# Conditioning vector spread by full-row products, first chunk's rows unsplit, output stores on other queues

## The chip, the cores and the metric

The kernel runs on one core of a Trainium2 chip. A core has a matrix engine (TensorE, PE in the profile; its weight loads are listed apart as PEld), a vector engine (VectorE, DVE), a scalar engine (ScalarE, ACT), a general engine (GpSimd, POOL) and a queueing engine (SyncE, SP). Transfers are issued on the queues of SP and ACT and carried by 16 DMA engines. The metric is the device time of one execution in microseconds (us), taken as the median of several runs.

## The reference

A decoder trunk of two layers over 256 tokens of width 1024, in float32. Each layer runs a half-step SwiGLU feed-forward block (FFN), a token mixer (attention in layer 0, a gated linear recurrence in layer 1) and a second FFN. Each of these sub-layers normalises its input and modulates it by a conditioning vector `c`:

```python
c_act = silu(c)
mod = (c_act @ mod_w[layer] + mod_b[layer]).reshape(B, 3, 3, D)
shift, scale, gate = mod[:, j, 0], mod[:, j, 1], mod[:, j, 2]
h = rmsnorm(x, g) * (1 + scale) + shift
x = x + w * (1 + gate) * sublayer(h)
```

Nothing of the first FFN can start before `silu(c)`, the first rows of `mod_w`, the row sums of squares of `x` and the first weights are there.

## The kernel before

**Layout.** `x` is kept transposed: eight chunks of 128 features by 256 tokens. Weights arrive in float32, and ACT and DVE split each piece into a high part `wh` (ACT copy, line 586) and a low part `wl` (DVE subtraction, line 589); PE then makes three products for each 128x128 block, high times high, high times low, low times high (line 616). Only the first chunk of the first FFN (k = 0) is multiplied unsplit, by float32 products (line 945).

**The order of the work.** Every operation is first recorded with a cost, its reads and its writes; `schedule` then makes one order for each engine from these costs and due times, and the program is issued in that order. Each engine executes its list in order, so an operation that waits holds all behind it on its engine. Loads go out on SP's queue in a written order (`first_order`): the two halves of `x`, then for each chunk k of the first FFN the rows of `mod_w` for scale (`m1`) and shift (`m0`) and the FFN's weights (`gu`). `m1`, `m0` and `gu` of a chunk are 512 KB, 512 KB and 1 MB.

**The head.** The first 13 us run as follows. PE fills the time with products of zeros (`warm`, line 1464: six at first, one in the middle, nine late). The conditioning vector comes by ACT's queue into `rawm`, as 8 rows of 128 numbers (`CR = 8`). PE spreads it over all 128 partitions: eight float32 products, each of one column of an identity matrix (`unit`, held at 8 rows) with the 8 rows (line 1481), four into each of two PSUM banks; ACT takes silu of each bank into one half of `cact` (512 columns). ACT and DVE square and add `x`; PE sums over the partitions with a matrix of ones (line 714); ACT makes `rms` by a logarithm and `rst` by an exponential.

Each row block of `mod_w` is multiplied by `cact` and summed along its row by one DVE instruction (line 650, 1024 columns, followed by a read of the accumulator). For k = 0 this is done in halves (`first_row`, line 916): two DVE instructions of 512 columns for `m1` and two for `m0`; ACT joins each pair (one instruction turns the first half's sum and the bias into `parts`, one adds the second half's sum). The result is the scale `mf` of chunk 0 and its shift.

Then DVE makes `hpre`, which is `x` times scale times `rst` (line 739), and a second tensor with the shift added (line 744, for the unsplit products: the two scalars are `parts` and the second half's raw sum). PE starts line 945, 16 logical products that the profile shows as 32 matmuls. ACT and DVE meanwhile make the split chunk 0 (`hx`) and all further chunks (lines 954, 967 and 969), for the products of k = 1 to 7 at line 616.

**The end.** After the last sub-layer PE sums the squares (line 1417) and ACT and DVE normalise the two halves of 128 tokens; DVE writes six pieces (lines 1434 and 1440), and each piece is stored when it is ready, by SP's queue (line 1445) or by ACT's (line 554), as the table `PUTS` says (half, first chunk, chunks, queue).

Of the kernel before, what the change touches and what calls it, by code (L numbers as in the profile page):

```python
# [39 lines left out]
EARLY, MID, LATE = 6, 1, 9  # L40
AHEAD = {(1, 0): 3}
KICK0, COPIED, PLAIN = (1, 4), (7,), 2
HXPAD, HKPAD, ARPAD = 112, 16, 88
SKIP = 1
PUTS = ((0, 0, 2, "SP"), (0, 2, 3, "SP"), (0, 5, 3, "SP"), (1, 0, 3, "ACT"), (1, 3, 3, "SP"), (1, 6, 2, "ACT"))
CR = 8
SCORES = 1450.0
VALUES = 1400.0

# [333 lines left out]
def first_order():  # L383

    yield "x", 0, 0, 4 * T
    yield "x", 4, 0, 4 * T + NP0
    for k in range(KD):
        for w in ("m1", "m0"):
            for a in range(0, D, D // 2 if k == 0 else D):
                yield w, k, a, D // 2 if k == 0 else D  # L390
        for a, n in zip(starts(k), pieces(k)):
            yield "gu", k, a, n

# [18 lines left out]
def trunk(ctx, tc, first_in, cb, par, modw, gu, wdn, qk, wv, wo, win, wri, wout, out):  # L412
# [88 lines left out]
    def fixed(name, cols, dt=F32):  # L501
        return const.tile([P, cols], dt, tag=name, name=name)
# [2 lines left out]
    x = [Buf(ap=xall[:, d * T : (d + 1) * T]) for d in range(KD)]  # L505
    cact = Buf(ap=fixed("cact", D))
    pars = Buf(ap=xall[:, KD * T :])
    zero = fixed("zero", 2 * P, BF16)
    pool.memset(zero, 0.0)
    eps_t = fixed("eps", 1)  # L510
# [10 lines left out]
    ident = fixed("ident", P, BF16)  # L521
    mask = fixed("mask", P)
    pool.affine_select(at[1][:, :P], ones, [[1, P]], ALU.is_equal, 0.0, base=0, channel_multiplier=-1)
    unit = at[1]
    dve.tensor_copy(ident, at[1][:, :P])
    pool.memset(mask, -NEG)
    pool.affine_select(mask, mask, [[1, P]], ALU.is_gt, NEG, base=0, channel_multiplier=-1)
# [8 lines left out]
    def col(off, n=1):  # L536
        return pars()[:, off : off + n]
# [4 lines left out]
                mraw[l, q, w] = Buf(ap=fixed(f"mr{l}{q}{w}", KD))  # L542
                mfin[l, q, w] = Buf(ap=fixed(f"mf{l}{q}{w}", KD))
    gbias = Buf(ap=fixed("gbias", KD))
    parts0 = [Buf(ap=fixed(f"parts{w}", 2)) for w in range(2)]
    shr = {(l, q): Buf(ap=fixed(f"sh{l}{q}", 2 * KD, F32R)) for l in range(2) for q in range(3) if l or q}
    fixed("pad1", ARPAD)

# [4 lines left out]
    def act_dma(dst, src, r, w, lat=2600.0):  # L553
        return pr.op("ACT", 60.0, lambda: act.dma_start(dst(), src() if callable(src) else src), r, w, lat=lat)
# [6 lines left out]
    def V(fn, n, r, w, cost=None, ptr=0, after=()):  # L561
        return pr.op("DVE", cost or c_dve(n) + 62.0 * ptr, fn, r, w, after)
# [171 lines left out]
    def norm_chunk(gen, d, q, whole=False):  # L734
        gs, sh = mfin[gen + (1,)], mfin[gen + (0,)]
        hp, hi, lo = Buf(hpr), Buf(hxr), Buf(hxr)
        hcur.setdefault(gen, []).append((hi, lo))
        c = slice(d, d + 1)
        V(lambda: dve.scalar_tensor_tensor(hp(), x[d](), gs()[:, c], q(), ALU.mult, ALU.mult), T,  # L739
          [x[d], (gs, d), q], [hp], ptr=1)  # L740
        h = None
        if whole:
            h, p, m = Buf(hpr), parts0[0], mraw[gen + (0,)]
            V(lambda: dve.tensor_scalar(h(), hp(), p()[:, 1:2], m()[:, c], ALU.add, ALU.add), T, [hp, (p, 1), (m, d)], [h], ptr=1)
        A(lambda: hi()[:, :T], hp, AF.Identity, T, [hp, (sh, d)], [hi], ptr=1, bias=lambda: sh()[:, c])
        V(lambda: dve.scalar_tensor_tensor(lo()[:, :T], hp(), sh()[:, c], f32(hi()[:, :T]), ALU.add, ALU.subtract), T,
          [hp, (sh, d), hi], [lo], ptr=1)
        lows[gen] = pr.ops[-1]
        return h
# [139 lines left out]
    def ffn(l, s, nxt, hook):  # L889
# [12 lines left out]
        if j == 0:  # L902
# [4 lines left out]

            gb, goff, boff = gbias, OFF_NG, OFF_MB

            def first_row(w):  # L910

                raw, m, f, p = Buf(rows, 8), mraw[0, 0, w], mfin[0, 0, w], parts0[w]
                for h in range(2):
                    cs, o = slice(h * D // 2, (h + 1) * D // 2), p if h == 0 else m
                    chained(lambda cs=cs: raw()[:, cs], at_[f"m{w}", 0, h * D // 2], D // 2, [(raw, h)], RATE0)
                    V(lambda cs=cs, o=o: dve.scalar_tensor_tensor(raw()[:, cs], raw()[:, cs], 1.0, cact()[:, cs], ALU.mult, ALU.mult,
                                                                  accum_out=o()[:, :1]),
                      D // 2, [(raw, h), (cact, h)] + [gbias] * (w == 1), [(raw, h), (o, 0)])
                    g = w == 1
                    first = lambda: gbias()[:, :1] if g else col(boff)  # L920
                    A(lambda h=h: f()[:, :1] if h else p()[:, 1:2], lambda o=o: o()[:, :1], AF.Identity, 1,
                      [(o, 0), (pars, 0), gbias] + [(p, 1)] * h, [(f, 0) if h else (p, 1)], ptr=1 + g,
                      scale=(lambda: col(goff)) if g else 1.0, bias=(lambda: p()[:, 1:2]) if h else first)

            def early(k, w):

                if k == KD:
                    return
                if k == 0:
                    first_row(w)  # L930
                    return
                last[:] = [mod_tile(0, 0, w, k, last, LAT0 if k < 3 + w else LAT1, RATE0, Buf(rows, 8))]
                m, f = mraw[0, 0, w], mfin[0, 0, w]
                mk, fk = (lambda: m()[:, k : k + 1]), (lambda: f()[:, k : k + 1])
                if w == 1:
                    A(fk, mk, AF.Identity, 1, [(m, k), (pars, 0), gb], [(f, k)], ptr=2, scale=lambda: col(goff + k),
                      bias=lambda: gb()[:, k : k + 1])
                else:
                    A(fk, mk, AF.Identity, 1, [(m, k), (pars, 0)], [(f, k)], ptr=1, bias=lambda: col(boff + k))
# [515 lines left out]
    def chained(dst, src, n, w, rate=RATE, lat=LAT0):  # L1455
        last[:] = [dma(dst, src, n, w, last, lat, rate)]
# [9 lines left out]

    def first_loads(F):
        c, b = Buf(modr), [Buf(banks), Buf(banks)]
        act_dma(lambda: c()[:CR, : D // CR], cb.rearrange("o (r n) -> (o r) n", r=CR), [], [c], 300.0)

        def cond(h, after=()):
            cs = slice(h * 512, (h + 1) * 512)
            A(lambda: cact()[:, cs], b[h], AF.Silu, 512, [b[h]], [(cact, h)], table="silu", psum=True, after=after)

        warm(EARLY)
        cw = D // CR
        for h in range(2):
            def fn(h=h):
                for r in range(h * CR // 2, (h + 1) * CR // 2):
                    o = r * cw - h * 512  # L1480
                    pe.matmul(b[h]()[:, o : o + cw], unit[:CR, r : r + 1].to_broadcast([CR, P]), c()[:CR, :cw], start=o == 0,  # L1481
                              stop=True, skip_group_check=True)
            pr.op("PE", 1870.0, fn, [c], [b[h]])
        warm(MID, [pr.last_pe])

        sq = [Buf(F, 8), Buf(F, 8)]
        extra = (0, NP0)
        tiles = {}
        for h in range(2):
            d, a0, n = 4 * h, 4 * h * T, 4 * T + extra[h]  # L1490
            chained(lambda a0=a0, n=n: xall[:, a0 : a0 + n], at_["x", d, 0], n, x[d : d + 4] + [(pars, 0)] * h, RATE0)

        def on_act(h, i):
            q, d = sq[h], 4 * h + i
            tiles[d] = (q, slice(i * T, (i + 1) * T), i)
            return A(lambda: q()[:, i * T : (i + 1) * T], x[d], AF.Square, T, [x[d]], [(q, i)])

        def on_dve(h, i):
            q, d = sq[h], 4 * h + i
            for e in range(2):  # L1500
                tiles[d + e] = (q, slice((i + e) * T, (i + e + 1) * T), "V")
            V(lambda: dve.tensor_tensor(q()[:, i * T : (i + 2) * T], xall[:, d * T : (d + 2) * T], xall[:, d * T : (d + 2) * T],
                                        ALU.mult), 2 * T, x[d : d + 2], [(q, "V")])

        on_dve(0, 2)
        on_act(0, 0)
        cond(0, [on_act(0, 1)])
        p, one = Buf(F, 4), Buf(F, 2)
        V(lambda: dve.tensor_tensor(p(), sq[0]()[:, : 2 * T], sq[0]()[:, 2 * T :], ALU.add), 2 * T,
          [(sq[0], "V"), (sq[0], 0), (sq[0], 1)], [p])  # L1510
        fold = V(lambda: dve.tensor_tensor(one(), p()[:, :T], p()[:, T:], ALU.add), T, [p], [one])
        on_dve(1, 0)
        on_act(1, 2)
        cond(1, [on_act(1, 3)])
        two = Buf(F, 2)
        V(lambda: dve.tensor_tensor(two(), sq[1]()[:, :T], sq[1]()[:, T : 2 * T], ALU.add), T, [(sq[1], "V")], [two])
        pairs = [tiles[6], (one, slice(0, T), None), tiles[7], (two, slice(0, T), None)]
        ssq[0, 0] = tuple(pairs)
        pr.op("DVE", 80.0, lambda: dve.scalar_tensor_tensor(gbias(), col(OFF_MB + KD, KD), 1.0, col(OFF_NG, KD), ALU.add,
                                                            ALU.mult), [(pars, 0)], [gbias], [fold])  # L1520
# [98 lines left out]
```

## Time and profile before

| what | value |
|---|---|
| median of 3 runs | 947.25 us (946.97 to 947.35) |
| the profiled execution, its own time | 946.62 us |
| its span, first to last instruction | 944.9 us |
| PE busy | 936.1 us, 99% of the span |
| DVE busy | 780.2 us, 83% |
| ACT busy | 559.9 us, 59% |
| first product of the first FFN (line 945) | starts at 12.61 us |
| last product | starts at 937.75 us |

A row of the profile names line, engine, operation and tiles (`out<-in`), then the count, the busy time and the mean duration. Matmuls overlap, so the duration of one is longer than the distance to the next. In the view that lists instructions in order of time a row begins with start and duration in us, and runs of the same instruction are merged (`x16`). The view of stretches gives for each engine the busy time and, in brackets, the number of instructions, then the clock granted to PE (1.00 or 0.50), the busy share of the DMA engines and their rate. That clock column holds recorded changes only; before the first of them it prints 1.00.

### The profile page before, as it was taken

Reading aid. Unit: us, or ns where it says so; the run is one execution under the profiler, and the core shown is the slowest. Engines: PE = TensorE matmul, PEld = TensorE weight load, DVE = VectorE, ACT = ScalarE, POOL = GpSimd, SP = SyncE. Lnnn points to the kernel's source line nnn. Section 1 sums busy time; section 2 is a strip of 40 time slices with the busy share of each in tenths; the row PEclk is TensorE's granted clock in tenths of the full one; section 3 lists DMA queues with packets and bytes.
Section 4 is the critical chain, followed back from the end, with each engine's and each line's share of the span. In section 5 each row is a group of like instructions: output and inputs, shape, how many; then the busy total and the mean of one; then the engine's idle time right before and its main releaser. Section 6 shows DMA issues by size and latency. Waiting matters only on the chain.

```text
span 944.9 us, 19631 instructions
## 1 busy us (share of the span) xinstructions
PE 936.1 (99%) x8092; PEld 926.9 (98%) x8092; DVE 780.2 (83%) x1250; ACT 559.9 (59%) x923; POOL 2.1 (0%) x14
## 2 busy tenths in 40 slices
PE   9999999999999999999999999999999999999997
PEld 7999999999999999999999999999999999999996
DVE  7999988799978998888899998866999997555444
ACT  6785453488776754554376544535789685544343
POOL 0000000000000000000000000000000000000000
PEclk9999999999999999999999999999999999999998
DMA  9989899947852888889967988886333656555531
GB/s 361 404 328 358 320 359 356 364 181 297 288 201 93 302 337 320 314 322 354 361 264 278 359 332 331 325 334 222 137 128 142 223 183 245 197 184 204 169 114 45
DMA packets 48777, 251.24 MB, mean 266 GB/s; under 512 B 5416, under 2 KB 6320, under 8 KB 28976
## 3 DMA queue, kind: packets, MB, share of 16 engines
q1 hardware_dynamic: 48384, 249.66, 71.0%
q8 instruction: 63, 1.03, 0.4%
q10 hardware_dynamic: 304, 0.33, 0.1%
q14 instruction: 26, 0.21, 0.1%
HBM read 248.92 MB, written 1.05 MB: 265 GB/s over the span
## 4 chain that ended last, share of the span: by engine, by line
PE 99%; DVE 0%; ACT 0%; issue 0%; POOL 0%; DVEq 0%; ACTq 0%; POOLq 0%
PE bank L616 92%; PE bank L1070 2%; PE bank L1303 1%; PE bank L945 1%; PE bank L1136 1%; PE bank L1197 1%; PE bank L1173 1%; PE bank L1481 0%; PE bank L714 0%; DVE raw L1434 0%; PE bank L1176 0%; PE bank L1464 0%; PE bank L1417 0%; PE bank L706 0%; ACT rms L558 0%
## 5 line engine op out<-in xcount | busy, mean ns | idle before, releaser
L616 PE MATMUL bank<-hx,wh 128*128 128x256 f32 (+1 forms) x3264 | 559.5, 277 | 0.0
L586 ACT ACTIVATE wh<-raw 128x1024 fp32r<-128x1024 f32 (+1 forms) x330 | 337.1, 1039 | 287.5 <-PE bank L616 213.8
L616 PEld LDWEIGHTS bank<-hx,wh 128*128 128x128 f32 x3264 | 493.0, 188 | 0.0
L589 DVE TENSOR_TENSOR wl<-raw,wh 128x1024 fp32r<-128x1024 f32 (+1 forms) x330 | 388.3, 1197 | 125.1 <-ACT wh L586 120.7
L616 PE MATMUL bank<-hx,wl 128*128 128x256 f32 (+1 forms) x1640 | 452.4, 277 | 0.0
L616 PEld LDWEIGHTS bank<-hx,wl 128*128 128x128 f32 x1640 | 308.1, 188 | 0.0
L616 PE MATMUL bank<-arenar,wh 128*128 128x256 f32 x1696 | 289.4, 276 | 0.0
L616 PEld LDWEIGHTS bank<-arenar,wh 128*128 128x128 f32 x1696 | 255.2, 188 | 0.3 <-issue 0.3
L616 PE MATMUL bank<-arenar,wl 128*128 128x256 f32 x848 | 234.2, 276 | 0.0
L616 PEld LDWEIGHTS bank<-arenar,wl 128*128 128x128 f32 x848 | 159.2, 188 | 0.1
L650 DVE SCALAR_TENSOR_TENSOR rawm<-rawm,cact 128x1024 f32<-128x1024 f32 x128 | 154.5, 1219 | 3.9 <-DMA rawm<-in_modw 3.8
L558 ACT ACTIVATE arenar<-a 128x256 fp32r<-128x256 f32 x88 | 35.3, 405 | 7.7 <-DVE a L882 7.6
L887 DVE TENSOR_TENSOR arenar<-a,arenar 128x256 fp32r<-128x256 f32 x88 | 36.4, 419 | 0.5 <-ACT arenar L558 0.5
L882 DVE TENSOR_TENSOR a<-bank,sg 128x256 f32<-128x256 f32 x82 | 34.1, 418 | 1.6 <-ACT sg L558 1.3
L558 ACT ACTIVATE sg<-bank 128x256 f32<-128x256 f32 x82 | 30.0, 369 | 7.2 <-PE bank L616 7.1
L558 ACT ACTIVATE arenaf<-bank 128x256 f32<-128x256 f32 (+1 forms) x53 | 22.9, 487 | 12.2 <-DVE bank L1146 4.5
L794 DVE SCALAR_TENSOR_TENSOR x<-bank,mf,x 128x256 f32<-128x256 f32 (+1 forms) x49 | 21.8, 473 | 9.1 <-PE bank L616 9.1
L558 ACT ACTIVATE hx<-x,mf 128x256 fp32r<-128x256 f32 x40 | 19.2, 502 | 15.6 <-DVE x L794 15.6
L558 ACT ACTIVATE hx<-hpre,mf 128x256 fp32r<-128x256 f32 x41 | 20.0, 503 | 8.4 <-DVE hpre L739 8.2
L1070 PE MATMUL bank<-wh,hx 128*128 128x256 f32 x128 | 23.5, 281 | 0.0
L1559 ACT ACT_TABLE_LOAD x15 | 19.2, 1283 | 1.6 <-PEq L1607 1.4
L1070 PEld LDWEIGHTS bank<-wh,hx 128*128 128x128 f32 x128 | 20.1, 189 | 0.1
(131 smaller groups left out, 510.6 us busy)
## 6 DMA issues: line engine op xcount, KB each, us to landing
raw<-in_gu SPq DMA_DIRECT2D x79, 1024.0 KB, 4.8
rawm<-in_modw SPq DMA_DIRECT2D x128, 512.0 KB, 6.5
raw<-in_wdn SPq DMA_DIRECT2D x44, 1024.0 KB, 5.1
raw<-in_win SPq DMA_DIRECT2D x10, 1024.0 KB, 4.8
raw<-in_qk SPq DMA_DIRECT2D x8, 1024.0 KB, 4.9
arenar<-in_first_in SPq DMA_DIRECT2D x14, 512.0 KB, 8.4
raw<-in_wout SPq DMA_DIRECT2D x5, 1024.0 KB, 4.9
raw<-in_first_in SPq DMA_DIRECT2D x8, 512.0 KB, 8.9
```

What stands on the lines that cost most here:

```text
L558: act.activation(o(), i(), f, **{k: (v() if callable(v) else v) for k, v in kw.items()})
L586: act.activation(h()[:, :m], raw()[:, a : a + m], AF.Copy)
L589: dve.tensor_tensor(lo()[:, :m], raw()[:, a : a + m], f32(h()[:, :m]), ALU.subtract)
L616: pe.matmul(o(b())[:, c], wc(u()), xc(v())[:, c], start=start and n == 0, stop=stop and n == len(passes) - 1, skip_group_check=True)
L650: dve.scalar_tensor_tensor(raw(), raw(), 1.0, cact(), ALU.mult, ALU.mult, accum_out=m()[:, t : t + 1])
L794: dve.scalar_tensor_tensor(x[d]()[:, w], acc.b()[:, j * T + w.start : j * T + w.stop], gate()[:, d : d + 1], x[d]()[:, w], ALU.mult, ALU.add)
L882: V(lambda: dve.tensor_tensor(a(), b()[:, T:], sg(), ALU.mult), T, [(b, (1, 0)), sg], [a])
L887: V(lambda: dve.tensor_tensor(y[1](), a(), f32(y[0]()), ALU.subtract), n, [a, y[0]], [y[1]])
L945: pr.op("PE", c_mm(T, 4), lambda: pe.matmul(b()[:, g * T : (g + 1) * T], raw()[:, c0 : c0 + P], h0(), start=start, stop=False, skip_group_ ...
L1070: pe.matmul(o, u()[:, tb * P : (tb + 1) * P], v()[:, c0 : c0 + 256], start=start and n == 0, stop=k == KD - 1 and n == 2, skip_group_check ...
L1136: pe.matmul(zb[e][i]()[:, j * m : (j + 1) * m], y()[rows, kc], y()[rows, qc], start=j == 0, stop=j == 1, skip_group_check=True)
L1559: act.preload_act_table_set(TABLES[t])
```

## The change

Five edits.

- The conditioning vector is loaded as one row of 1024 numbers into the last partition of its tile. DVE sets the other 127 partitions of that tile to zero ahead of everything else on its list. PE spreads the vector with two float32 products of the full 128-row matrix of ones, 512 columns each, in place of eight products of 8 rows and 128 columns.
- For k = 0, `m1` and `m0` are loaded whole (one transfer of 512 KB each in place of two of 256 KB) and reduced by one DVE instruction of 1024 columns each, with one ACT instruction behind each, like the other chunks. `first_row` and its `parts` tiles go.
- Line 744 keeps its shape, but adds the raw sum of `m0` and the bias column as its two scalars.
- A padding tile grows by 16 columns where the `parts` tiles went.
- The stores of four of the six output pieces change queues. The order by piece was SP, SP, SP, ACT, SP, ACT and becomes SP, SP, ACT, SP, ACT, SP.

```diff
-HXPAD, HKPAD, ARPAD = 112, 16, 88
+HXPAD, HKPAD, ARPAD = 112, 16, 104
-PUTS = ((0, 0, 2, "SP"), (0, 2, 3, "SP"), (0, 5, 3, "SP"), (1, 0, 3, "ACT"), (1, 3, 3, "SP"), (1, 6, 2, "ACT"))
-CR = 8
+PUTS = ((0, 0, 2, "SP"), (0, 2, 3, "SP"), (0, 5, 3, "ACT"), (1, 0, 3, "SP"), (1, 3, 3, "ACT"), (1, 6, 2, "SP"))
...
-        for w in ("m1", "m0"):
-            for a in range(0, D, D // 2 if k == 0 else D):
-                yield w, k, a, D // 2 if k == 0 else D
+        yield "m1", k, 0, D
+        yield "m0", k, 0, D
...
+    dve.memset(modt[0][: P - 1, :], 0.0)
...
-            h, p, m = Buf(hpr), parts0[0], mraw[gen + (0,)]
-            V(lambda: dve.tensor_scalar(h(), hp(), p()[:, 1:2], m()[:, c], ALU.add, ALU.add), T, [hp, (p, 1), (m, d)], [h], ptr=1)
+            h, m = Buf(hpr), mraw[gen + (0,)]
+            V(lambda: dve.tensor_scalar(h(), hp(), m()[:, c], col(OFF_MB + d), ALU.add, ALU.add), T, [hp, (m, d), (pars, 0)], [h],
+              ptr=1)
...
-            def first_row(w):
...
-                if k == 0:
-                    first_row(w)
-                    return
-                last[:] = [mod_tile(0, 0, w, k, last, LAT0 if k < 3 + w else LAT1, RATE0, Buf(rows, 8))]
+                last[:] = [mod_tile(0, 0, w, k, last, LAT0 if k < 3 + w else LAT1, RATE0, Buf(rows, 8), [gbias] if k == w == 0 else [])]
...
-        act_dma(lambda: c()[:CR, : D // CR], cb.rearrange("o (r n) -> (o r) n", r=CR), [], [c], 300.0)
+        act_dma(lambda: c()[P - 1 :, :], cb, [], [c], 300.0)
...
-                for r in range(h * CR // 2, (h + 1) * CR // 2):
-                    o = r * cw - h * 512
-                    pe.matmul(b[h]()[:, o : o + cw], unit[:CR, r : r + 1].to_broadcast([CR, P]), c()[:CR, :cw], start=o == 0,
-                              stop=True, skip_group_check=True)
-            pr.op("PE", 1870.0, fn, [c], [b[h]])
+            pr.op("PE", 1870.0, lambda h=h, cs=cs: pe.matmul(b[h]()[:, :], ones, c()[:, cs], start=True, stop=True),
+                  [c], [b[h]])
```

More of the change, by code (lines that the diff above doesn't have):

```diff
@@ L523, in trunk @@
     pool.affine_select(at[1][:, :P], ones, [[1, P]], ALU.is_equal, 0.0, base=0, channel_multiplier=-1)
-    unit = at[1]
     dve.tensor_copy(ident, at[1][:, :P])
@@ L544, in trunk @@
     gbias = Buf(ap=fixed("gbias", KD))
-    parts0 = [Buf(ap=fixed(f"parts{w}", 2)) for w in range(2)]
     shr = {(l, q): Buf(ap=fixed(f"sh{l}{q}", 2 * KD, F32R)) for l in range(2) for q in range(3) if l or q}
@@ L908, in ffn @@
             gb, goff, boff = gbias, OFF_NG, OFF_MB
-            def first_row(w):
[L912 to L923, printed above, removed]
             def early(k, w):
@@ L1475, in first_loads @@
         warm(EARLY)
-        cw = D // CR
         for h in range(2):
-            def fn(h=h):
-                for r in range(h * CR // 2, (h + 1) * CR // 2):
-                    o = r * cw - h * 512
-                    pe.matmul(b[h]()[:, o : o + cw], unit[:CR, r : r + 1].to_broadcast([CR, P]), c()[:CR, :cw], start=o == 0,
-                              stop=True, skip_group_check=True)
-            pr.op("PE", 1870.0, fn, [c], [b[h]])
+            cs = slice(h * 512, (h + 1) * 512)
+            pr.op("PE", 1870.0, lambda h=h, cs=cs: pe.matmul(b[h]()[:, :], ones, c()[:, cs], start=True, stop=True),
+                  [c], [b[h]])
         warm(MID, [pr.last_pe])
```

## The prediction

> **What bounds the kernel now.** I read the page first (spans, engine shares, chain of waits), then the chain in order of time for the head, then single lines and stretches for the clock.
>
> ```profile
> span 944.9 us, 19631 instructions
> PE 936.1 (99%) x8092; PEld 926.9 (98%) x8092; DVE 780.2 (83%) x1250; ACT 559.9 (59%) x923; POOL 2.1 (0%) x14
> PE 99%; DVE 0%; ACT 0%; issue 0%; POOL 0%; DVEq 0%; ACTq 0%; POOLq 0%
> ```
>
> PE carries the chain from end to end, so an edit counts only where it moves the start of PE's long stream, makes PE wait in it, or changes what follows its last product. The chain's view of the first 40 us (start, length, what) shows where the stream starts.
>
> ```profile
> 1.16 1.46 PE bank L1464 x6
> 2.62 3.71 PE bank L1481 x16
> 6.66 3.43 PE bank L714 x8
> 10.18 0.47 ACT rms L558
> 11.54 0.49 DVE hpre L739
> 12.14 0.42 DVE hpre L744
> 12.61 7.17 PE bank L945 x32
> 20.07 16.43 PE bank L616 x144
> ```
>
> PE spreads the vector (L1481), sums squares (L714), then waits for rms, rst, scale and two DVE steps, and starts L945 at 12.61. From there it runs without a gap. The clock matters in this head: the views of single lines give the shortest, median and longest duration in ns; the view of stretches follows.
>
> ```profile
> L1481 PE MATMUL bank<-rawm,a x16: 416/416/574, 2.6 to 5.9; 8*128 8x128 f32 x16
> L714 PE MATMUL bank<-arenaf,ones x8: 634/634/634, 6.5 to 9.4; 128*128 128x256 f32 x8
> L945 PE MATMUL bank<-hpre,raw x32: 379/379/483, 12.6 to 19.4; 128*128 128x256 f32 x32
> L1464 PE MATMUL bank<-zero x16: 273/421/421, 1.2 to 11.5; 128*128 128x256 bf16 x16
> ...
> 937.75 0.28 PE L1417 MATMUL bank<-sq,ones 128*128 128x128 f32 x1
> ...
> 4.66:8.07 3.41, 3.41 (x13) 2.92 (x13) 3.23 (x9) 3.15 (x6) 0.00 (x0) 1.00 0.98 370
> 8.07:11.48 3.41, 3.41 (x13) 2.34 (x13) 1.66 (x6) 1.50 (x6) 0.00 (x0) 1.00 1.01 413
> 936.49:939.90 3.41, 1.54 (x13) 1.26 (x11) 1.96 (x6) 2.25 (x7) 0.00 (x0) 1.00 0.01 2
> 939.90:944.90 5.00, 0.00 (x0) 0.00 (x0) 1.55 (x5) 0.00 (x0) 0.00 (x0) 0.50 0.60 208
> ```
>
> L714 and L945 have one shape, yet 634 against 379 ns; by their distances in the chain 0.43 against 0.224 us. So the head runs at half clock. Only the last zero product of L1464, at 11.5, drops to 273 ns: the clock rose at about 11.48, although PE had been occupied since 1.16. Before that rise stand 3.41 us (that length is my choice) of products over all 128 rows; the stretch before it, equally occupied, held 8-row products until about 6.2 and the clock stayed low. I read it so: products of 8 rows hardly count as activity. The clock fell again at 939.90 after a stretch in which PE was occupied for 1.54 of 3.41 us, 45%, its last product starting at 937.75.
>
> The Trainium skill, "TensorE: Matmul & The Clock Gate", Part 1, has the clock released after one window of about 3.4 us of sustained activity and says nothing of rows; by that the rise would have come by 8 us at the latest. The trace's 11.48 disagrees, so the measurement decides.
>
> **The change part by part.** The sum is made against the profiled execution's own 946.62 us; the median of the runs lies 0.63 higher, and 0.2% of it, 1.9 us, is about what a measurement of this kernel can tell from no change.
>
> ```profile
> 0.79 0.58 ACTq L554 DMA_DIRECT2D rawm<-in_cb  x1
> 1.22 0.32 POOL L515 MEMSET a<- 128x256 f32 x1
> 1.94 0.44 DVE L518 CAST ntri<-a 128x128 fp32r<-128x128 f32 x1 [1.94 <-POOL a L516]
> 6.78 0.42 DVE L1516 TENSOR_TENSOR arenaf<-arenaf 128x256 f32<-128x256 f32 x1
> 6.99 1.28 ACT L1559 ACT_TABLE_LOAD   x1
> 9.65 0.08 DVE L916 DVE_READ_ACCUMULATOR arenar<-arenar,cact 128x1 f32 x1
> 10.55 0.38 ACT L558 ACTIVATE parts<-parts,gbias,x 128x1 f32<-128x1 f32 x1
> 10.83 0.40 ACT L558 ACTIVATE rst<-rms 128x256 f32<-128x256 f32 x1
> 13.21 1.22 DVE L650 SCALAR_TENSOR_TENSOR arenar<-arenar,cact 128x1024 f32<-128x1024 f32 x1
> 14.35 0.08 DVE L650 DVE_READ_ACCUMULATOR arenar<-arenar,cact 128x1 f32 x1
> L916 DVE SCALAR_TENSOR_TENSOR arenar<-arenar,cact x4: 684/684/685, 7.2 to 9.0; 128x512 f32<-128x512 f32 x4
> L650 DVE SCALAR_TENSOR_TENSOR arenar<-arenar,cact x14: 1217/1220/1226, 13.2 to 46.0; 128x1024 f32<-128x1024 f32 x14
> ```
>
> *The zeroing on DVE.* No row has it. Below, POOL's 0.32 us for a quarter of the columns; above, four times that, 1.3 us. I take 1.2, near the DVE pass of 1024 columns (1.22). DVE's list was idle until 1.94, and PE is in its zero products until 2.62: nothing on the path. Without that cover (end after 2.6) its excess would go straight onto the head. The casts queued behind it (L518) could slip by 0.1; the chain has no row of theirs.
>
> *One row instead of eight.* Same 4 KB, one issue on ACT's queue (0.58) as before. Its landing has no row; the smallest transfers that have one, the stores below, take 2.0. At worst it lands at 2.8, 0.2 late; at best nothing is gained, PE being in its zero products. I take 0.
>
> *The products.* 16 matmuls of 128 columns become 4 of 512: the same columns, 3.7 us at half clock; fewer seams save 0.2 at most. I take 0.
>
> *The clock.* Now the time from 1.16 on is full-row products. In this execution's phase I expect the rise at 4.66 instead of 11.48. L714 then costs 8 x 0.224 = 1.8 instead of 3.43, but its last operand (L1516) ends at 7.20, so its last pair ends at about 7.75. ACT's table load ends at 8.27. So rms starts at 8.30 instead of 10.18: 1.88 earlier.
>
> *The whole rows.* Two passes of 1.22, starting 1.14 apart (as 13.21 and 14.35), replace four of 0.68: DVE ends at 7.20 + 2 x 1.14 + 0.17 = 9.65, where it ended at 9.73. The `parts` instruction of 0.38 goes; it lay between rms and rst, and rst waits for rms anyway: 0 (0.3 at best). hpre follows rms by 11.54 - 10.18 = 1.36, so 9.66, and DVE has it at 9.75. L945 follows hpre by 1.07: **10.82 instead of 12.61, 1.79 earlier.** Two transfers fewer save SP issue time; the DMA engines are 98 to 101% busy there, so the landings stay. Line 744's other scalar has the same shape: 0.
>
> *What the early clock loses.* The nine late zero products now run at full clock, some 1.0 us, and end at 8.75; PE then stands empty until 10.82. In 8.07 to 11.48 it is occupied 0.68 + 0.66 = 1.34 of 3.41 us, 39%; the stretch that lost the clock had 45%. So I expect the clock to fall at 11.48 and return at 14.90. L945 needs 7.17 us at full clock: 0.66 are done by 11.48, 1.71 in the 3.42 us at half, the other 4.80 end at 19.70. Before, 12.61 + 7.17 = 19.78. **Of 1.79 us, 0.08 remain.**
>
> *The stores.* The rows are SP's issues, DVE's last write, and the times from issue to landing, of SP's queue first, then of ACT's.
>
> ```profile
> L1445 SPq DMA_DIRECT2D out<-raw x4: 332/340/354, 939.0 to 941.0; - x4
> ...
> 941.10 0.35 DVE L1440 SCALAR_TENSOR_TENSOR raw<-x,rst 128x128 f32<-128x128 f32 x1
> DMA to landing us min/median/max: 2.0/2.2/2.4
> DMA to landing us min/median/max: 2.1/2.1/2.1
> ```
>
> The last piece (128 KB) went out by ACT's queue and took 2.1; SP's 128 KB store took 2.0. I take -0.1, between -0.1 and +0.3. SP's queue needs 0.34 for an issue, less than DVE for the next piece, so nothing queues there.
>
> *The padding* keeps later addresses: 0.
>
> Sum: 0.08 + 0.1 = 0.2 us faster than 946.62, or **947.0 us** in the median.
>
> **The rivals.** *A, the clock stays high through the gap.* Speaking for it: 39% is near the 45%, the threshold may lie lower, and another phase of the stretches would split the gap between two. The Trainium skill, same page, table at its end, asks only that no gap exceed about 3 us; by that rule the 2-us gap keeps the clock and A comes true. The trace disagrees: last product at 937.75, clock down at 939.90. Here L945 ends 1.79 earlier, but not all survives, because ACT's splits wait for transfers.
>
> ```profile
> ACT wh L586 <- DMA raw<-in_first_in: 5.4, 6, 1.7
> 40.92 1.07 ACT L586 ACTIVATE wh<-raw 128x1024 fp32r<-128x1024 f32 x1
> 42.02 2.54 DVE L589 TENSOR_TENSOR wl<-raw,wh 128x1024 fp32r<-128x1024 f32 x2
> 36.54 13.47 PE bank L616 x118
> ```
>
> At 144 matmuls in 16.43 us a chunk of 48 takes 5.48; k = 4 starts at 36.3 and k = 5's second half at 44.5, in A at 42.7. Its `wl` is the first of the pair at 42.02 and ends at 43.25, held by a transfer. PE waits 0.55, so 1.24 remain: 947.25 - 1.24 - 0.1 = 945.9.
>
> *B, rows do not count* and the clock rises at 11.48 as before (something else held it). Then only seams are gained: 946.9. Against it speaks the occupied but cold stretch 4.66 to 8.07.
>
> *C, slower: the clock is lost and PE starts late.* If the early clock comes, but the new order holds L945 back to about 12.4 (a row of `mod_w` or another DVE pass put ahead of hpre), the gap takes the rest of the stretch, the clock falls at 11.48, and 2.5 of the next 3.41 us are filled. If that isn't enough for a rise, PE is at half clock until 18.31: 5.9 us do 2.95 of the 7.17, the rest ends at 22.5, 2.75 later than before: 949.9. With the rise at 14.90 it is +1.0, 948.2. It decides at a start of L945 after about 11.5.
>
> **How the numbers follow.** My forecast 0.37, A 0.20, B 0.13, C 0.30. The forecast's own range is 946.5 to 947.5 by the small bounds above. A ends inside 0.2% unless its stall is absent (945.36 is the limit), 0.08 for faster; of C's chance, in which other harm from a reordered plan is counted, 0.25 lies above 949.14: slower; the rest, 0.67, is no change. The 8-in-10 range from 945.3 to 949.9 reaches from A to the worse end of C.
>
> **What would show it.** Durations of L714 near 380 ns instead of 634 show the early clock; the start of L945 near 10.8 the shorter head; 483 ns or more in L945's middle, and a recorded 0.50 from 11.5 to 14.9, the loss. A shows L945 all at 379 and a wait of `wl` near 42. B shows L714 at 634 still. I am wrong if PE waits somewhere after 50 us, where I count on an unchanged order, or if L1481 starts later than 2.8.

## The result, and the profile after

The changed kernel takes 945.47 us in the median (22 runs); the kernel before took 947.16 beside it (22 runs). The ratio is 0.9981, with a 95% interval of 0.9974 to 0.9987: faster by 1.7 us, at the edge of what a measurement of this kernel can tell from no change. Repeated in a second series, the same kernel gave 946.0 against 946.56, ratio 0.9995 (0.9986 to 1.0004), an interval that holds 1. Single executions 6 us or more above the rest occur with several kernels, the one before among them; they stand in the ratios and intervals, so a ratio can lie above 1 where the median is lower.

The profiled execution took 945.19 us against 946.62, 1.43 less. Line numbers have moved: the spread is line 1458 (was 1481), the square sums 711 (714), the first plain products 925 (945), the split products 613 (616), the zero products 1444 (1464), the two steps of `hpre` 736 and 741 (739 and 744). First the page:

```profile
span 943.5 us, 19596 instructions
...
PE 933.9 (99%) x8080; PEld 923.5 (98%) x8080; DVE 781.1 (83%) x1247; ACT 558.5 (59%) x921; POOL 2.1 (0%) x14
...
PE 99%; DVE 0%; DMA 0%; ACT 0%; issue 0%; DVEq 0%; ACTq 0%
```

PE still carries the chain. What is new is a DMA at its head. The chain in order of time (start, length, what):

```profile
0.79 2.37 DMA rawm<-in_cb
...
3.29 3.75 PE bank L1458 x4
7.05 0.21 PE bank L1444
7.26 2.10 PE bank L711 x8
...
9.45 0.47 ACT rms L555
...
10.54 0.50 DVE hpre L736
...
11.06 0.42 DVE hpre L741
...
11.52 7.17 PE bank L925 x32
```

The single lines (shortest, median, longest in ns; first and last start):

```profile
L506 DVE MEMSET rawm<- x1: 912/912/912, 1.1 to 1.1; 127x1024 f32 x1
L1458 PE MATMUL bank<-rawm,ones x4: 1061/1062/1194, 3.3 to 6.0; 128*128 128x512 f32 x4
L711 PE MATMUL bank<-arenaf,ones x8: 379/380/636, 7.1 to 9.0; 128*128 128x256 f32 x8
L925 PE MATMUL bank<-hpre,raw x32: 379/379/483, 11.5 to 18.3; 128*128 128x256 f32 x32
```

The square sums are at 380 ns, which was 634: the clock rose at 7.85, before at 11.48. But the spread starts at 3.29 where it started at 2.62 on the chain (2.56 by its first record), because the vector's one row lands about 0.7 us later. So L925 starts at 11.52 instead of 12.61: **1.09 us earlier**. `rms` accounts for 0.73 of that (9.45 against 10.18); the rest lies between `rms` and L925, where `hpre` now follows `rms` by 1.09 instead of 1.36 and its second step follows after 0.52 instead of 0.60. PE's rows around the gap in front of it:

```profile
7.05 2.29 PE L711 MATMUL bank<-arenaf,ones 128*128 128x256 f32 x8
9.18 1.15 PE L1444 MATMUL bank<-zero 128*128 128x256 bf16 x9
11.52 0.70 PE L925 MATMUL bank<-hpre,raw 128*128 128x256 f32 x2 [1.20 <-DVE hpre L741]
```

PE is empty for 1.2 us only (9.18 + 1.15 = 10.33 to 11.52). The clock's recorded rise and fall mark the ends of stretches of 3.41 us. Here are the two stretches ahead of the rise, the one behind it and the end (PE's busy time stands third; the granted clock is the third number from the end; ahead of the rise at 7.85 it is half speed, though 1.00 is printed):

```profile
1.02:4.44 3.41, 2.60 (x8) 1.39 (x9) 1.48 (x5) 1.29 (x2) 1.63 (x10) 1.00 0.75 258
4.44:7.85 3.41, 3.41 (x7) 1.56 (x6) 2.97 (x6) 2.67 (x7) 0.00 (x0) 1.00 1.01 376
7.85:11.26 3.41, 2.48 (x16) 1.83 (x14) 3.03 (x7) 2.52 (x6) 0.00 (x0) 1.00 1.03 421
...
939.69:943.48 3.79, 0.00 (x0) 0.00 (x0) 0.60 (x3) 0.00 (x0) 0.00 (x0) 0.50 0.54 195
```

The stretch with the gap is filled by 2.48 of 3.41 us, 73%, and the clock stays at 1.00 until 939.69 in this execution. L925 takes 7.17 us, as before, and the 1.09 us survive: compared product by product, PE is 1.09 ahead at 57.8 us and 1.15 at its last product.

```profile
936.60 0.28 PE L1397 MATMUL bank<-sq,ones 128*128 128x128 f32 x1
```

From there to the end of the span it is 943.48 - 936.60 = 6.88 us; before it was 944.9 - 937.75 = 7.15. Sum: 1.15 of the head and 0.27 of the end make 1.42 of the 1.43 us.

So three questions: is it the rows in use that raise the clock earlier (theory R), or another part of the change? What limits the gain of the head? And does a gap before L925 lose the clock at all?

### The profile page after: what moved, and what is told of

It is laid out like the page before. It is cut to its first block, busy times and chain, and to the rows that moved or that the text cites. A ratio compares the mean times of both kernels' runs of the same rounds, so it can differ in the third digit from the quotient of the medians.

```text
span 943.5 us, 19596 instructions
## 1 busy us (share of the span) xinstructions
PE 933.9 (99%) x8080; PEld 923.5 (98%) x8080; DVE 781.1 (83%) x1247; ACT 558.5 (59%) x921; POOL 2.1 (0%) x14
## 3 DMA queue, kind: packets, MB, share of 16 engines
HBM read 248.92 MB, written 1.05 MB: 265 GB/s over the span
## 4 chain that ended last, share of the span: by engine, by line
PE 99%; DVE 0%; DMA 0%; ACT 0%; issue 0%; DVEq 0%; ACTq 0%
PE bank L613 92%; PE bank L1050 2%; PE bank L1283 1%; PE bank L925 1%; PE bank L1116 1%; PE bank L1177 1%; PE bank L1153 1%; PE bank L1458 0%; DMA rawm<-in_cb 0%; PE bank L711 0%; DVE raw L1414 0%; PE bank L1156 0%; PE bank L1397 0%; PE bank L703 0%; ACT rms L555 0%; ACT rst L555 0%
```

## The experiments

### The parts alone

**Stores alone.** The kernel before, with the new `PUTS` only:

```diff
-PUTS = ((0, 0, 2, "SP"), (0, 2, 3, "SP"), (0, 5, 3, "SP"), (1, 0, 3, "ACT"), (1, 3, 3, "SP"), (1, 6, 2, "ACT"))
+PUTS = ((0, 0, 2, "SP"), (0, 2, 3, "SP"), (0, 5, 3, "ACT"), (1, 0, 3, "SP"), (1, 3, 3, "ACT"), (1, 6, 2, "SP"))
```

> The kernel before with the stores alone moved between the queues. Theory R (the rows of the spreading products release the clock early, and that carries the gain): only the end moves, about 0.2 us faster (946.9), first product of the first FFN still at 12.6 us. Rival S (the stores carry the gain): about 1.4 us faster, 945.7.

Measured: 947.12 us (before beside it 946.82), ratio 1.0015 (0.9993 to 1.0037). The square sums stay cold (single line), and the end gains nothing (the list in order of time, its head and the last product):

```profile
L714 PE MATMUL bank<-arenaf,ones x8: 380/634/634, 6.7 to 9.5; 128*128 128x256 f32 x8
```

```profile
core 0 of [0], span 946.9 us
...
939.73 0.28 PE L1417 MATMUL bank<-sq,ones 128*128 128x128 f32 x1
```

946.94 - 939.73 = 7.21 us, no less than before's 7.15. The queues are not what shortened the end. (This execution took 948.68: between 195 and 202 us its PE fell back by 2.4 us against the kernel before, which the median does not show.)

**All but the spread.** The changed kernel with the vector landing and spread as before:

```diff
+CR = 8
-    dve.memset(modt[0][: P - 1, :], 0.0)
-        act_dma(lambda: c()[P - 1 :, :], cb, [], [c], 300.0)
+        act_dma(lambda: c()[:CR, : D // CR], cb.rearrange("o (r n) -> (o r) n", r=CR), [], [c], 300.0)
-            pr.op("PE", 1870.0, lambda h=h, cs=cs: pe.matmul(b[h]()[:, :], ones, c()[:, cs], start=True, stop=True),
+                    pe.matmul(b[h]()[:, o : o + cw], unit[:CR, r : r + 1].to_broadcast([CR, P]), c()[:CR, :cw], start=o == 0,
```

> The changed kernel with the vector spread by 8-row products again (whole first rows, two scalars and stores kept). R: the squares' sums (now 128x256, float32) take 634 ns again, the first product of the first FFN starts at 12.2 to 12.6 us, and the time is 946.7 to 947.0, some 1.4 us behind the changed kernel. Rival W (the whole rows and the missing instructions on ACT carry the gain): still about 945.5.

Measured: 946.0 against 946.82, ratio 0.9990 (0.9978 to 1.0002).

```profile
L712 PE MATMUL bank<-arenaf,ones x8: 634/634/634, 6.4 to 9.4; 128*128 128x256 f32 x8
L926 PE MATMUL bank<-hpre,raw x32: 379/379/483, 12.2 to 19.0; 128*128 128x256 f32 x32
```

Without the new spread the square sums are cold again. L926 starts at 12.24, 0.37 earlier than before the change; `rms` and `rst` start as before (10.17 and 10.82), but `hpre` follows `rst` by 0.44 instead of 0.71. That is the worth of the whole rows in the head, which the prediction had bounded at 0.3 and taken as 0: from `rms` to the first product it is 2.42 or 2.43 us in four traces with split rows and 2.07 in three with whole rows. This start was not kept either: in this execution, which took 947.14, PE waited 0.73 us at 45 us for the `wl` of k = 5's second half, and at 57.8 us it was 0.83 behind the kernel before. The end is the short one, 6.89.

**The spread alone.** The kernel before with the single row, the zeroing and the two full-row products:

```diff
+    dve.memset(modt[0][: P - 1, :], 0.0)
-        act_dma(lambda: c()[:CR, : D // CR], cb.rearrange("o (r n) -> (o r) n", r=CR), [], [c], 300.0)
+        act_dma(lambda: c()[P - 1 :, :], cb, [], [c], 300.0)
-                    pe.matmul(b[h]()[:, o : o + cw], unit[:CR, r : r + 1].to_broadcast([CR, P]), c()[:CR, :cw], start=o == 0,
+            pr.op("PE", 1870.0, lambda h=h, cs=cs: pe.matmul(b[h]()[:, :], ones, c()[:, cs], start=True, stop=True),
```

> The kernel before with the one-row vector and the two full-row products alone. R: the spreading starts at 3.3 us instead of 2.6, yet the first product of the first FFN starts near 11.5 and the time is 1.1 to 1.3 us shorter, about 946.0. W: the late landing is all that is left, 0 to 0.7 us slower.

Measured: 945.93 against 946.82, ratio 1.0005 (0.9984 to 1.0026).

```profile
L1478 PE MATMUL bank<-rawm,ones x4: 671/1061/1191, 2.8 to 5.5; 128*128 128x512 f32 x4
L714 PE MATMUL bank<-arenaf,ones x8: 379/379/473, 6.1 to 7.7; 128*128 128x256 f32 x8
L945 PE MATMUL bank<-hpre,raw x32: 379/379/483, 10.6 to 17.4; 128*128 128x256 f32 x32
```

The early clock is there, and L945 starts 1.99 us earlier, since the row landed for a spread at 2.81 in this execution. But of the 1.99 only 0.54 are left at 57.8 us: PE waits between 30 and 57 us, 0.55 us of it at the start of k = 4.

### Rows in use

**All 128 rows, same transfer, same columns.** The kernel before, its eight rows of 512 B landing in partitions 120 to 127 of a zeroed tile, and the same 16 products over 128 rows:

```diff
+    dve.memset(modt[0][: 128 - CR, : D // CR], 0.0)
-        act_dma(lambda: c()[:CR, : D // CR], cb.rearrange("o (r n) -> (o r) n", r=CR), [], [c], 300.0)
+        act_dma(lambda: c()[128 - CR : 128, : D // CR], cb.rearrange("o (r n) -> (o r) n", r=CR), [], [c], 300.0)
-                    pe.matmul(b[h]()[:, o : o + cw], unit[:CR, r : r + 1].to_broadcast([CR, P]), c()[:CR, :cw], start=o == 0,
+                    pe.matmul(b[h]()[:, o : o + cw], unit[:128, 128 - CR + r : 128 - CR + r + 1].to_broadcast([128, P]), c()[:128, :cw], start=o == 0,
```

> The kernel before with its 8 rows landing in partitions 120 to 127 of a zeroed tile, spread by eight products over all 128 rows: same transfer, same columns, only the rows of the array differ. R: spreading starts at 2.6 us, the clock rises 3 to 6 us earlier, the first product starts near 10.9 to 11.3 and the time is 1.2 to 1.7 us shorter, unless the clock falls again in the gap behind the late zero products (then about 0). A rival in which the number of matmuls or the one row matters, not the rows in use: no change.

Measured: 945.94 against 946.82, ratio 0.9992 (0.9970 to 1.0013).

```profile
L1482 PE MATMUL bank<-rawm,a x16: 364/421/553, 2.7 to 6.1; 128*128 128x128 f32 x16
L715 PE MATMUL bank<-arenaf,ones x8: 379/379/382, 6.4 to 7.9; 128*128 128x256 f32 x8
L946 PE MATMUL bank<-hpre,raw x32: 379/379/483, 10.8 to 17.6; 128*128 128x256 f32 x32
```

The products are as many and as long as in the kernel before (421 against 416 ns); only the rows differ. The clock rose at 6.24, the square sums are warm, L946 starts at 10.81. That shows R. It shows the next limit as well, in the chain at k = 4:

```profile
34.42 0.83 issue
35.25 0.08 DVE arenar L651
35.33 0.34 DVE hx L970
35.68 0.04 issue
35.72 24.34 PE bank L617 x212
```

PE waits for `hx`. On DVE it stands behind a pass over a row of `mod_w`, and that behind a `wl`, whose `wh` on ACT had waited 1.67 us for a transfer of weights. `hx` comes at 35.25, almost when it came before the change (35.32), so the earlier PE has to wait for it. The wait takes 0.48 us; of 1.80 at the start 1.02 are left at the last product.

**Half the rows.** The same with 64 rows:

```diff
-        act_dma(lambda: c()[128 - CR : 128, : D // CR], cb.rearrange("o (r n) -> (o r) n", r=CR), [], [c], 300.0)
+        act_dma(lambda: c()[64 - CR : 64, : D // CR], cb.rearrange("o (r n) -> (o r) n", r=CR), [], [c], 300.0)
```

> The kernel before with its eight rows landing in partitions 56 to 63 of a zeroed tile and the 16 spread products over 64 rows: half the rows in use, the same columns. If the rows in use weigh in the clock's activity, 64 rows at half clock fill a stretch only by half of what 128 rows do, so the clock rises as late as with 8 rows (9.5 to 12.5), the square sums stay at 634 ns and L945 starts at 12.2 to 12.6. If only a handful of rows is too few, the rise comes at 5.5 to 8, the square sums take 380 ns and L945 starts at about 10.8.

Measured in a single execution: 946.75 (before beside it 947.29).

```profile
L1482 PE MATMUL bank<-rawm,a x16: 417/417/579, 2.6 to 5.9; 64*128 64x128 f32 x16
L715 PE MATMUL bank<-arenaf,ones x8: 380/634/636, 6.5 to 9.4; 128*128 128x256 f32 x8
L946 PE MATMUL bank<-hpre,raw x32: 379/379/483, 12.3 to 19.1; 128*128 128x256 f32 x32
```

64 rows are not enough: the clock rose at 9.35, so the stretch from 2.53 to 5.94, full of 64-row products, did not raise it, and the next one, mostly of full rows, did. L946 starts at 12.31. It is not that a handful is too few; the rows in use weigh. Numbers between 64 and 128 were not tried.

### The landing, the end, the gap

Four kernels on one chip; before beside them 946.56 (33 runs). The changed kernel once more, as yardstick:

> The changed kernel itself, once more, as the yardstick of the three beside it. Theory R (the rows in use decide whether the early products count for the clock): the clock rises at 4.7 to 8, L925 starts at 11.5 instead of 12.6, last product to span end 6.9 instead of 7.1: about 1.4 us under the kernel before, more where the profile shows no wait in the stream. Rival (the gain seen first was the state of one chip): no difference beyond 0.3 us.

Measured: 946.0, ratio 0.9995 (0.9986 to 1.0004). In its profiled execution the row landed early: the spread starts at 2.42, the square sums end at 7.94, and L925 starts at 11.00. What holds it there is no longer `rms`, by the chain:

```profile
1.71 5.83 DMA arenar<-in_first_in
...
7.64 1.23 DVE arenar L647 x2
...
8.95 1.14 DVE arenar L647 x2
10.10 0.41 DVE hpre L736
```

The two whole-row passes stand ahead of `hpre` on DVE, and the first waited for its transfer until 7.54. L925 is 1.62 us earlier than before the change, but waits from 36 to 57 us leave 0.67, and 0.38 at the last product. The gap ahead of L925, from 8.92 to 11.00, has the length that the prediction had drawn, 2.07 us; the end of a stretch at 9.27 shared it out, the two were filled by 90% and 50%, and the clock stayed.

**Eight rows landing, 128 rows in use**, in the changed kernel:

```diff
-        act_dma(lambda: c()[P - 1 :, :], cb, [], [c], 300.0)
+        act_dma(lambda: c()[128 - CR : 128, : D // CR], cb.rearrange("o (r n) -> (o r) n", r=CR), [], [c], 300.0)
```

> The changed kernel with the vector landing as eight rows of 512 B in partitions 120 to 127 and eight products over all 128 rows. If the single 4096-B packet is what made the spread start 0.73 late, the spread starts at 2.6 to 2.8 instead of 3.3 and L925 at about 10.8 instead of 11.5; the transfers then no longer run ahead of PE, so a wait of about 0.5 us at k = 4 or 5 takes most of it back: 0.2 to 0.3 us under the changed kernel. If the cover holds: 0.7 under it. If the late landing was not on the path: no difference.

Measured: 946.12, ratio 0.9997 (0.9988 to 1.0005), no better than its yardstick. The spread starts at 2.85 and L927 at 10.78, 1.83 earlier than before the change, but 1.05 remain at 57.8 us, after waits at the same place (k = 4). So a better landing buys a start that the transfers take back.

**Store queues of before**, in the changed kernel (the diff of the stores, backwards):

> The changed kernel with the store queues of before (last store by ACT's queue). If the queue of the last store gives the end's gain, last product to span end goes from 6.87 back to about 7.15 and the time up by 0.25 to 0.3 us. If the two transfers fewer in the head give it (another order of the closing waits), it stays at 6.9 and the time is the same within 0.1.

Measured: 945.78, ratio 0.9993 (0.9984 to 1.0002).

```profile
core 0 of [0], span 943.2 us
...
936.43 0.28 PE L1397 MATMUL bank<-sq,ones 128*128 128x128 f32 x1
```

943.25 - 936.43 = 6.82 us: the end is short with the old queues too. Counted from the start of the last product, SP's first closing step behind the last landing starts at 5.84 before the change, 5.91 with the new queues alone, 5.94 in the changed kernel and 5.88 here: SP's queue gains nothing. What differs comes behind. SP has six waits left behind that landing in the kernel before and with the stores alone, three in the changed kernel and here; and ACT's last closing step, at 6.79 to 6.93 before, is over by 6.44 now. Two transfers fewer at k = 0 may shift which semaphore the last store signals; that cause is argued. What is shown are the two sets of ends: 7.1 to 7.3 us in all profiled executions with split rows, 6.8 to 7.0 in all with whole rows, whatever the queues.

**A longer gap.** The changed kernel with one late zero product:

```diff
-EARLY, MID, LATE = 6, 1, 9
+EARLY, MID, LATE = 6, 1, 1
```

> The changed kernel with one late zero product instead of nine, so that PE is empty from about 9.4 to 11.5, 2.1 us instead of 1.3: about the gap that the prediction had counted with. By the prediction's step (a stretch of 3.4 us filled under 45% loses the clock) 1.3 of 3.4 us are filled where the gap lies in one stretch, so the clock is lost in about a third of the executions, and those take 1.4 to 1.7 us longer; L925 then shows 483 to 640 ns in its middle. By the rival (a gap of 2 us keeps the clock wherever it lies) all executions stay within 0.3 us of the changed kernel and L925 stays at 379 ns.

Measured: 946.05, ratio 0.9996 (0.9987 to 1.0005); the times form no group apart from the yardstick's (945.13 to 947.24 against 945.16 to 947.35). The two stretches from the rise on, in the profiled execution:

```profile
7.46:10.87 3.41, 1.56 (x8) 1.04 (x6) 2.88 (x7) 2.39 (x5) 0.00 (x0) 1.00 1.02 413
10.87:14.28 3.41, 2.97 (x14) 2.64 (x15) 2.88 (x7) 0.90 (x2) 0.00 (x0) 1.00 1.02 409
```

A stretch filled by 1.56 of 3.41 us, 46%, kept the clock there, over a gap of 2.30 us.

The profile shows one execution; the record has the mean granted clock of each, and there the loss does appear. Behind its last fall each trace shows 1.5 to 5.0 us at half clock, which makes a mean of 0.997 to 0.999. A mean of 0.996 takes at least 6.6 us at half clock, so some of it lies elsewhere. It is on record for 3 of the 11 executions here, for 1 of 11 of the yardstick, 2 of 11 with eight rows landing, 4 of 11 with the store queues of before, and for 1 of the 22 of the changed kernel behind the result, its slowest (947.21). None of the 100 executions of the kernel before that ran beside these experiments is under 0.997, nor are the 24 of the two kernels with the early clock and split rows. With the store queues of before the four took 946.70 to 947.04 us and the other seven 944.97 to 945.92, so the loss is worth about 1.3 us there; here the three (946.05 to 946.33) lie among the others. No trace of such an execution is at hand: that the clock is lost in the gap before L925 is the reading that fits, and the filled gap below, where none of 11 executions is under 0.998, speaks for it.

**A gap of a whole stretch, and its partner.** Five idle ACT passes ahead of the first `rst`, and the nine late zero products replaced by one (gap) or by 28 (filled); the planner sees the same costs in both:

```diff
+    pad1, slow = fixed("pad1", ARPAD), [5]
-        A(o, r, AF.Exp, T, [r], [o], table="lnexp", scale=-0.5)
+        pr.op("ACT", c_act(T, False, 0), lambda n=slow.pop() if slow else 0: ([act.activation(pad1, zero[:, :ARPAD], AF.Copy) for _ in range(n)], act.activation(o(), r(), AF.Exp, scale=-0.5)), [r], [o], (), "lnexp")
-            for _ in range(n):
+            for _ in range(1 if n == LATE else n):
```

> The changed kernel with five idle ACT passes of 104 columns ahead of the first rst (about 1.3 us) and one late zero product in place of nine, so that PE is empty from about 9 to 12.3, some 3.2 us: rival C's late start with the prediction's gap. By the prediction's step (a stretch of 3.4 us filled under about 45% loses the clock) most phases of the stretches lose it: the record shows 0.50 for one stretch from about 11 on, L925 has 483 to 640 ns in its middle, its 32 products take 8.9 us instead of 7.2, and the median lies 1.2 to 1.7 us above its partner with the gap filled. By the rival (only a gap longer than a whole stretch loses the clock) L925 stays at 379 ns and the two have one median.

> The same five idle ACT passes, with 28 zero products in place of the late nine, so that the same 3.2 us are filled. Both theories: the clock stays, L925 starts at about 12.3 with 379 ns, 0.8 later than in the changed kernel, and the time is about that of the kernel before less 0.3 of the head and 0.3 of the end: 0.5 us under it.

Measured: with the gap 948.79, filled 946.94, before beside them 947.29. The runs with the gap fall into three groups: 946.45 to 946.85 (3), 948.42 to 948.98 (5), 950.24 and 950.37; the filled ones all lie from 945.69 to 947.44. The profiled execution with the gap took 946.85, of the first group, and kept its clock over a gap from 9.52 to 13.04:

```profile
8.01:11.42 3.41, 1.51 (x8) 0.99 (x6) 2.46 (x5) 2.75 (x7) 0.00 (x0) 1.00 1.02 408
11.42:14.83 3.41, 1.79 (x8) 1.61 (x9) 2.74 (x7) 1.29 (x4) 0.00 (x0) 1.00 1.03 410
```

The gap was split between two stretches, filled by 44% and 52%. The mean granted clock tells the groups apart: 0.999 in the first, 0.994 to 0.997 in the second, 0.994 in the third, and 0.994 takes 10.4 us or more at half clock, two stretches beside the end. So seven of these ten lost the clock, but no trace of theirs was at hand. The gap was therefore made longer, with nine passes:

```diff
-    pad1, slow = fixed("pad1", ARPAD), [5]
+    pad1, slow = fixed("pad1", ARPAD), [9]
```

> The kernel with one late zero product and nine idle ACT passes in place of five, so that PE is empty for about 4.7 us and L925 starts at 14.2, 1.6 later than before the change. Whatever the phase, one stretch of 3.4 us is then filled by at most a third. If the clock is lost by how far a stretch is filled (the prediction's step), the record shows 0.50 after a rise near 6 to 9, part of L925 runs at 483 to 640 ns and its 32 products take 8.9 us (one stretch) or 10.6 us (two) instead of 7.2; time 949.5 to 952, never near 948. If the three clusters seen with the gap of 3.2 us (946.6, 948.7, 950.3) are something else than the clock, the record stays at 1.00, L925 at 379 ns, and the time is 1.6 above the kernel before, less 0.3 at the end: 948.2.

Measured: 948.41 (948.1 to 950.45), ratio 1.0019 (0.9999 to 1.0038); profiled execution 948.25. In stretches of the recorded clock:

```profile
6.00:9.41 3.41, 2.21 (x11) 1.45 (x9) 3.38 (x7) 3.30 (x8) 0.00 (x0) 1.00 1.03 418
9.41:12.82 3.41, 0.00 (x0) 0.00 (x0) 1.02 (x4) 2.76 (x11) 0.00 (x0) 1.00 1.02 409
12.82:16.24 3.41, 3.19 (x8) 2.56 (x9) 3.41 (x7) 1.23 (x3) 0.00 (x0) 0.50 1.04 397
16.24:19.65 3.41, 3.41 (x17) 3.03 (x16) 3.41 (x9) 2.97 (x7) 0.00 (x0) 1.00 1.06 404
```

```profile
L925 PE MATMUL bank<-hpre,raw x32: 379/379/796, 13.0 to 21.4; 128*128 128x256 f32 x32
```

This is the loss that the prediction had drawn: after an empty stretch the clock is 0.50 for exactly one stretch, L925 reaches 796 ns, and PE goes from 0.44 us behind the kernel before to 1.99 behind: 1.55 us for the stretch. All nine executions have a mean granted clock of 0.997 or 0.994. The time missed the expected 949.5 to 952, as the kernel before took 946.48 in this series: 946.48 + 1.99 - 0.3 at the end is 948.2, which is also what the other theory had named for a clock that stays, so here the recorded clock decides and not the time. By the Trainium skill, "TensorE: Matmul & The Clock Gate", Part 1 (its table of states), the clock goes down after one idle window of about 3.4 us; this stretch agrees, but the kernel before lost it after a stretch filled by 45%.

## Why the prediction was right or wrong

The forecast of no change holds by luck. The kernel came out 1.7 us faster, just under the 1.9 us that the prediction had called no change; the forecast's own range, 946.5 to 947.5, does not hold 945.47, and the wide one, from 945.3, holds it by 0.2. What came is the course of rival A, which had 0.20.

**The early clock: right.** The square sums went from 634 to 380 ns, and the experiments with 128 and 64 rows show that the rows in use are the reason. The instant was off (7.85, not 4.66), and not because of the phase: a stretch ended at 4.44, but PE had filled only 2.60 of its 3.41 us, 76%, as the spread waited for its row until 3.29, and the clock stayed low. In all ten traces with products of 128 rows the rise came at the end of the first stretch that PE filled by 94% or more; stretches of up to 81% ahead of it did not raise it. Whether the products of zeros in these count in full is open. Over the traces the rise came between 5.64 and 8.01 with products of 128 rows (ten), and between 9.33 and 11.48 with fewer (four). The limit of 8 us that the prediction drew from the Trainium skill, "TensorE: Matmul & The Clock Gate", Part 1, holds with all rows in use and fails with 8 or 64.

**One row instead of eight: mis-sized.** Taken as 0, at worst 0.2; it measured 0.73 in the profiled execution (3.29 against 2.56), and PE stood empty for 0.67 us in the first stretch. In others of the same spread it started at 2.42, 2.81 and 3.35, so the cost is between nothing and 0.8. The start of 10.82 that the prediction worked out for a landing at the old time came true in the kernel that had it (split rows, eight rows landing, 128 in use: 10.81).

**What the early clock loses: the step that failed.** "So I expect the clock to fall at 11.48", from a stretch filled by 39% in a gap of 2.07 us. In the profiled execution of the changed kernel the square sums ended later and so did the zero products, the gap was 1.2 us, the stretch was filled by 73%, and nothing was lost, and by a mean granted clock of 0.998 or 0.999 the same holds for 21 of the 22 executions. The limit was wrong too: 45% had lost the clock at the end of the kernel before, while 44% and 46% kept it in the head. The mechanism is real (0.50 on record with nine idle passes), but the prediction took for certain what only some executions show: by the mean of 0.996, 1 of 22 of the changed kernel, and 1 to 4 of 11 of the kernels of the second series. In the traces, gaps up to 2.3 us kept the clock, one of 3.5 us kept it (3 of 10 executions of that kernel by their times and clocks), and one of 4.8 us lost it. The rule of the Trainium skill that the prediction set beside it ("TensorE: Matmul & The Clock Gate", table at its end: no gap beyond about 3 us) agrees with the traced gaps, but not with the executions at 0.996, if theirs were as short as the traced ones. With this step the forecast fell from 1.79 to 0.08 us.

**Rival A is what came**, at 1.09 instead of 1.24 us of head. Its limit, a wait of 0.55 us for a transfer, is real but mostly stands elsewhere: at k = 4, for `hx` (0.3 to 0.55 us in five traces). The `wl` of k = 5's second half showed as 0.73 us in the kernel without the new spread and as 0.3 us or less in three others. The changed kernel on record lost nothing there; where it started 1.62 earlier, 0.67 were left. Of starts 1.3 to 2.0 us earlier, between 0.4 and 1.3 were left at 57.8 us, and of the 0.37 without the new spread nothing: so the landings of an execution count beside the start. That the gain of the whole change was 1.7 us in one series and 0.6 in the other fits this, and more lost stretches in the second (at least 1 of 11, against 1 of 22) may add to it; how far late landings, a late rise of the clock and its loss each make that difference was not separated.

**Rival B** fell with the 380 ns. **Rival C** needed a start of L925 after about 11.5; it came at 11.52, but with the zero products ending at 10.33 the gap never opened.

**Stores: mis-sized, and for the wrong reason.** -0.1 was taken, between -0.1 and +0.3; it measured -0.27, and the queues have no part in it: behind the last landing SP goes on 0.06 to 0.07 later with them, and the end is shorter in every trace with whole rows.

**Whole rows: 0 was wrong by up to 0.37**, a third of the changed kernel's 1.09; where everything else is early they can also become the bound themselves (L925 at 11.00, behind two passes). **Zeroing**: 0.91 us against 1.2, hidden as said. **After 50 us**: nothing moved, as counted on.

## What to carry to other kernels

Early products that are to raise PE's clock should use all its rows; here products over 8 or 64 rows kept PE occupied and left it at half speed for another stretch. A gap of 1 to 2 us ahead of the first long stream cost only itself in every trace, but the mean granted clock shows a lost stretch in some executions: look at all executions, not only at the profiled one, and count such a loss as a chance, which was seven in ten with the gap of 3.5 us and nine in nine with the longer one. Before counting an earlier start as gained, compare it with the next transfers: here starts 1.3 to 2.0 us earlier were worth 0.4 to 1.3 us at 57.8 us.

## What had not been expected of the hardware

- The single row of 4096 B is one packet of 1006 ns in the changed kernel's trace and 614 ns in that of the spread alone, and between 201 and 1091 ns over eight traces; the eight packets of 512 B before took 25 ns each. The spread behind the one row started between 2.42 and 3.35 us (eight traces), behind eight rows between 2.55 and 2.85 (six): the long row lands less evenly, in three of the eight later than any of the six.
- The clock changes only at the ends of stretches of 3.413 us that have their own phase in each execution: from rise to fall it was 928.43 us before and 931.84 after, 272 and 273 stretches, and in every other trace a whole number too. The Trainium skill, "TensorE: Matmul & The Clock Gate", Part 1, calls the window free-running; the traces agree.
- How far a stretch is occupied does not decide alone whether the clock stays: 44% and 46% kept it in the head, 45% and (at the end of the kernel with one late zero product, 1.64 of 3.41 us) 48% lost it, and 49% kept it at the end of the kernel with eight rows landing (1.67 of 3.41 us). What else weighs beside the rows, the columns or the type of the products, stays open.
